# The short first load of an adaptive max-pool kernel, issued as two DMAs of 64 partitions from SyncE and ScalarE

## The chip, the cores and the metric

The kernel runs on one core of a Trainium2 chip. The metric is the device time of one execution in microseconds (us); lower is better. The profile shows the same execution from its first to its last instruction (the "span", some 1.8 us shorter). When the text speaks of "packet records", it means the list of single DMA packets in the trace, with start, duration, size and queue; the DMA engine is not recorded, so I give counts and means over all 16.

## The reference

The input has shape 32 x 256 x 4096, fp32 (134.22 MB). Each output is the maximum of 16 neighbouring values.

```python
for i in range(output_size):                 # 256
    start = int(i * length / output_size)    # 4096 / 256 = 16 values each
    end = int((i + 1) * length / output_size)
    result[:, :, i] = np.max(x[:, :, start:end], axis=-1)
```

There is one comparison for each value loaded, so the question is how fast 134 MB come in.

## The kernel before

The rows are spread over 128 partitions. A window is the 16 values of one output. SyncE loads chunks of 1024 windows per partition (8 MiB, 64 KiB to a partition) by turns into two places of one buffer, `ring`; each place is shifted by 152 windows for every second load into it. VectorE reduces each chunk in two parts, so that the place comes free early. The very first load is short: 128 windows, 1 MiB, 8 KiB to a partition. It lies in the gap between the two places.

```python
CHUNK, GAP, FIRST = 1024, 152, 128
...
ring = pool.tile([P, 2 * (CHUNK + GAP) * W], fp32, ...)     # W = 16
...
for n in loads:                    # 128, 1024, 1024, ... , the last 900
    xn = xg[:, a * W : (a + n) * W]
    if n == FIRST:
        nc.sync.dma_start(
            out=ring[:, CHUNK * W : (CHUNK + n) * W], in_=xn
        )
        pooled(dst, CHUNK, n)
    else:
        low = n_loads % 2 * (CHUNK + GAP)
        moved = n_loads // 2 % 2
        at = low + moved * GAP
        nc.sync.dma_start(out=ring[:, at * W : (at + n) * W], in_=xn)
        ...                        # two reductions, of 872 and 152 windows
...
nc.scalar.dma_start(out=og[:, full : full + last], in_=last_kept)
...                                # two larger stores, from SyncE
```

## Time and profile before

| what | value | where it is read |
|---|---|---|
| time | 334.97 us (334.9 to 335.02, 3 runs) | timed runs |
| DMA engines, SyncE's queue | 98.8% of the span | DMA queues |
| VectorE | 83% of the span | busy time |
| first DMA packet | 1.744 us | packet records |
| last DMA packet ends | 331.836 us | packet records |
| first reduction | 5.40 us, then 17.07 us of waiting | timeline |

The lines behind the table, and what they say of the bound, are in the prediction.

### The profile page before, as it was taken

How to read it: one execution, taken by the hardware profiler on the slowest of the kernel's cores; microseconds unless marked ns; L12 is line 12 of the kernel's file. 1: busy time of each engine (PE TensorE's matmuls, PEld its weight loads, DVE VectorE, ACT ScalarE, POOL GpSimd, SP SyncE). 2: the span in 40 equal slices, each digit the busy share in tenths (PEclk: the TensorE clock that was granted, in tenths of full speed). 3: DMA queues.
4: the chain of work that ended last, by engine and by line, in shares of the span. 5: the costliest groups of instructions: out<-in, count | busy, mean ns of one | idle time of the engine just before them, and what ended most of it. 6: DMA issues, size and time to landing. Idle time of an engine off the chain costs nothing.

```text
span 333.2 us, 113 instructions
## 1 busy us (share of the span) xinstructions
DVE 276.5 (83%) x32; POOL 0.2 (0%) x4
## 2 busy tenths in 40 slices
DVE  2009979797997979799797979979797998979993
POOL 0000000000000000000000000000000000000000
DMA  9898989899898989899898989899898989899987
GB/s 378 378 504 378 504 378 504 378 409 472 378 504 378 504 378 504 378 417 464 376 502 377 504 378 496 386 425 456 378 504 378 504 378 504 378 458 443 393 386 339
DMA packets 2880, 142.61 MB, mean 428 GB/s; under 512 B 320, under 2 KB 320, under 8 KB 448
## 3 DMA queue, kind: packets, MB, share of 16 engines
q1 hardware_dynamic: 2736, 142.15, 98.8%
q10 hardware_dynamic: 144, 0.46, 0.3%
HBM read 134.22 MB, written 8.39 MB: 428 GB/s over the span
## 4 chain that ended last, share of the span: by engine, by line
DMA 57%; DVE 36%; DVEq 5%; issue 0%; SPq 0%
DMA ring<-in_x_dram 57%; DVE kept L56 36%; DVEq L145 5%; SPq L85 0%
## 5 line engine op out<-in xcount | busy, mean ns | idle before, releaser
L56 DVE TENSOR_REDUCE kept<-ring 128x152 f32<-128x2432 f32 (+3 forms) x31 | 261.4, 8473 | 51.6 <-DMA ring<-in_x_dram 51.6
L56 DVE TENSOR_REDUCE ring<-ring 128x900 f32<-128x14400 f32 x1 | 15.1, 15141 | 0.0
L131 POOL MEMSET const-bfloat16-1.0<- 128x1 bf16 x1 | 0.1, 102 | 0.0
L131 POOL MEMSET const-uint8-127<- 128x1 uint8 x1 | 0.1, 101 | 0.0
L131 POOL MEMSET const-float32-0.0<- 128x1 f32 x1 | 0.1, 99 | 0.2 <-issue 0.2
L131 POOL MEMSET const-float32-1.0<- 128x1 f32 x1 | 0.1, 98 | 0.0
## 6 DMA issues: line engine op xcount, KB each, us to landing
ring<-in_x_dram SPq DMA_DIRECT2D x1, 8160.0 KB, 24.0
ring<-in_x_dram SPq DMA_DIRECT2D x1, 7200.0 KB, 21.6
out_dram<-kept SPq DMA_DIRECT2D x1, 4670.0 KB, 32.4
out_dram<-kept SPq DMA_DIRECT2D x1, 3072.0 KB, 18.1
ring<-in_x_dram SPq DMA_DIRECT2D x1, 1024.0 KB, 4.6
out_dram<-ring ACTq DMA_DIRECT2D x1, 450.0 KB, 4.2
ring<-in_x_dram SPq DMA_DIRECT2D x14, 24.0
```

The lines of the kernel that those rows point to most:

```text
L56: nc.vector.reduce_max(out=dst, in_=ring[:, at * W : (at + n) * W].rearrange("p (n w) -> p n w", w=W), axis=mybir.AxisListType.X,)
L131: nc = _bacc.Bacc("TRN2", target_bir_lowering=False, num_devices=1)
L145: with _tile.TileContext(nc) as tc:
```

## The change

The intent is to bring the short first load in sooner by issuing it from two engines at once, each for half of the partitions.

```diff
-                nc.sync.dma_start(
-                    out=ring[:, CHUNK * W : (CHUNK + n) * W], in_=xn
-                )
+                half = P // 2
+                for queue, h in ((nc.sync, slice(0, half)), (nc.scalar, slice(half, P))):
+                    queue.dma_start(
+                        out=ring[h, CHUNK * W : (CHUNK + n) * W], in_=xn[h]
+                    )
                 pooled(dst, CHUNK, n)
```

## The prediction

> **What bounds the kernel now.** I read the page first, then the table of busy time by stretches, then the chain of waits in order of time, then the timeline of the start and of one load in the middle. The page gives the shares:
>
> ```profile
> span 333.2 us, 113 instructions
> DVE 276.5 (83%) x32; POOL 0.2 (0%) x4
> DMA  9898989899898989899898989899898989899987
> q1 hardware_dynamic: 2736, 142.15, 98.8%
> HBM read 134.22 MB, written 8.39 MB: 428 GB/s over the span
> DMA ring<-in_x_dram 57%; DVE kept L56 36%; DVEq L145 5%; SPq L85 0%
> ```
>
> The transfers of the SyncE queue occupy the 16 DMA engines for 98.8% of the span, VectorE only 83%. The chain (last line) gives 57% to the loads and 36% to the reductions, which reads as if a faster reduction would help. The tail of the timeline says otherwise (start, length, what):
>
> ```profile
> 257.06 17.28 DVE L56 TENSOR_REDUCE kept<-ring 128x872 f32<-128x13952 f32 x2 [2.08 <-DMA ring<-in_x_dram]
> 271.77 19.68 SPq L94 DMA_DIRECT2D ring<-in_x_dram  x2
> 276.41 17.28 DVE L56 TENSOR_REDUCE kept<-ring 128x872 f32<-128x13952 f32 x2 [2.07 <-DMA ring<-in_x_dram]
> 295.75 17.28 DVE L56 TENSOR_REDUCE kept<-ring 128x872 f32<-128x13952 f32 x2 [2.07 <-DMA ring<-in_x_dram]
> ```
>
> A load lands every 19.35 us (276.41 - 257.06), VectorE works 17.28 of them and waits 2.07. The load issued at 271.77 lands at 295.73, 24 us later, though the rate is one per 19.35: for its first 4.6 us (to 276.41) it stands behind the load before it, whose landing starts the reduction at 276.41. So the DMA queue never runs dry, and the chain's reductions hide behind that backlog. The stretches (length, VectorE busy, POOL busy, clock, DMA share, GB/s) confirm it:
>
> ```profile
> 1.00:1.70 0.70, 0.00 (x0) 0.00 (x0) 1.00 0.00 0
> 1.70:5.00 3.30, 0.00 (x0) 0.00 (x0) 1.00 1.59 616
> 5.00:24.40 19.40, 2.29 (x1) 0.00 (x0) 1.00 1.01 436
> 63.00:295.70 232.70, 207.29 (x24) 0.00 (x0) 1.00 1.00 434
> 312.80:328.10 15.30, 15.29 (x2) 0.00 (x0) 1.00 0.99 428
> 331.90:333.20 1.30, 0.00 (x0) 0.00 (x0) 1.00 0.00 0
> ```
>
> (A packet counts in the stretch where it starts, hence 1.59 in the second row.) The engines are idle until 1.74 us, then saturated to 331.84 us, the end of the last packet. The time is therefore: start of the first packet (1.74), plus the DMA engines' work (330.1), plus the closing (1.3). A change counts only if it moves the first packet, or adds or removes DMA engine time.
>
> The first load, in the packet records of the trace: 128 packets of 8,192 B, eight per engine. The first packets start between 1.744 and 2.283 us and take 0.55 to 0.94 us, nearly all later ones 0.309 us (26.5 GB/s). The engines pass to the 64 KiB packets of the next load between 4.675 and 5.003 us; those take 2.418 us (27.1 GB/s). No gap lies between the two loads. Its consumer is far from critical:
>
> ```profile
> 0.73 0.38 SPq L85 DMA_DIRECT2D ring<-in_x_dram  x1
> 5.40 2.29 DVE L56 TENSOR_REDUCE kept<-ring 128x128 f32<-128x2048 f32 x1 [5.40 <-DMA ring<-in_x_dram]
> 24.75 17.28 DVE L56 TENSOR_REDUCE kept<-ring 128x872 f32<-128x13952 f32 x2 [17.07 <-DMA ring<-in_x_dram]
> ```
>
> VectorE starts on it at 5.40 and then waits 17.07 us for the next load.
>
> [...]one issue took 0.383 us on SyncE and 0.374 us on ScalarE, and the second SyncE issue already hides behind the first load. [...]The trace before has transfers of 128 partitions only, at 434 GB/s[...].
>
> **The change part by part.**
>
> Removed: half of the first SyncE transfer. The issues measured take 0.33 to 0.43 us whatever the size, so I save nothing there. SyncE's issue should still start at 0.73 and its next one near 1.16.
>
> Added: one issue on ScalarE, about 0.37 us. ScalarE is let go by the start barrier at 0.652, SyncE at 0.648, so the two go out together. Its later wait, for the final reduction, is untouched. Added too: 16 semaphore packets of 9 ns, one per engine: 0.01 us. The first reduction now waits for two semaphores, with 17 us of slack.
>
> Moved: the 1 MiB reaches each engine as two rings of four 8 KiB packets[...]. Bytes and data packets are unchanged. The first packet should still start at about 1.74, since it follows the SyncE issue. With no other effect the sum is 0.00 + 0.01 = no change: 335.0.
>
> [...]The engines' first packets are staggered by 0.31 us (15 of them, 1.744 to 2.055). Two engines half that list apart start some 0.16 us apart, which is half a packet. [...]As the engines never idle afterwards (the backlog above), such a delay goes to the end in full. Sum: 0.00 (issue) + 0.01 (semaphores)[...] = +0.9 us, so 334.97 + 0.9 = 335.9 us.[...]
>
> **The rivals.**
>
> Nothing moves. The queues alternate packet by packet[...].[...] The time is 334.9 to 335.1. I give it about 30%.
>
> Full serialization. The SyncE half goes first[...], the ScalarE half follows[...].[...] Against: from its fifth packet on, SyncE's ring already holds the 128-partition load[...]. The time is 336.8 to 337.4. About 20%.
>
> A faster start. The first packets cost 0.55 to 0.94 instead of 0.309 us. If the queues' start-ups overlap, or if ScalarE's is quicker, 0.1 to 0.4 us come off: 334.6 to 334.9. Against: the start-up is paid per engine, and all 16 are started by one issue already. About 12%.
>
> A late ScalarE half. If its small packets alternate with 64 KiB ones, each waits 2.4 us and the half lands after 10 to 14 us instead of 5.4. The first reduction starts late, but ends well before 24.7, and the third load, which overwrites this region, is issued only near 39.5. No change in the time by itself; it can go with any of the others.
>
> **Range and chances.** The lower end is a faster start of 0.3 us, the upper end full serialization: 334.6 to 337.3, centre 335.9. The runs before lie within 0.12 us, so noise is small. The 2% line is 6.7 us. The first load occupies the engines for 3.3 us in all, so even losing it whole or tripling it scarcely gets there. Chances: faster 0.005, same 0.99, slower 0.005.
>
> **What would show each step right or wrong.** The first packet stays within 0.1 us of 1.74 (issue saves nothing). The 8 KiB packets take clearly more than 0.309 us, 0.4 to 0.6[...]; if they stay at 0.309,[...] the time should be 335.0. The first 872-wide reduction, now at 24.75, starts 0.9 us later, and the same shift appears at 257.06, 276.41 and 295.75. VectorE still waits about 2.07 us ahead of each load. The queue of ScalarE carries about 1 MB instead of 0.46 MB, still under 1% share. The prediction is wrong if the shift at the start differs from the shift at the end, or if a later load loses its backlog.

The sum came to +0.9 us, 335.9 us in all. Its terms were 0.00 for the issue, 0.01 for the semaphores and 0.9 for slower 8 KiB packets. That third term was an estimate of mine, which started from eight packets at twice 0.309 us (+2.47 us, as a ceiling), took off the stagger of 0.16 us at each packet (+1.2 us left), and from that a quarter for the start-up (0.9). The doubling was not shown before the change; most of the changed kernel's packets later took 0.50 to 0.65 us. The 0.4 to 0.6 us named at the end of the prediction has the same ground.

## The result, and the profile after

The changed kernel took 337.47 us (median of 6 runs, 337.38 to 337.54) against 334.97 us: 2.50 us more. The ratio is 1.0074 (95% interval 1.0061 to 1.0087). Ratios here are the mean time of one kernel's runs over that of the other's in the same rounds, so they are not quite the ratio of the medians quoted. The loss is clear of the noise, below 2%, and 0.17 us above the upper end of the predicted range.

The page of the changed kernel, the lines that answer to the first fence of the prediction:

```profile
span 335.7 us, 116 instructions
DVE 276.5 (82%) x32; POOL 0.2 (0%) x4
DMA  8898989898989899998989898989898999999997
q1 hardware_dynamic: 2672, 141.62, 98.0%
q10 hardware_dynamic: 224, 0.99, 1.1%
HBM read 134.22 MB, written 8.39 MB: 425 GB/s over the span
DMA ring<-in_x_dram 58%; DVE kept L56 36%; DVEq L147 5%; SPq L87 0%
```

Same bytes, same VectorE time, still 99.1% of the engines' span (98.0 + 1.1; before, 98.8 + 0.3): yet the span is 2.5 us longer. So the DMA engines were busy for longer with the same bytes. Only a small part of the loss, 0.31 us, is a later start (below).

The timeline of the start (start, length, engine and line, what):

```profile
0.73 0.55 SPq L87 DMA_DIRECT2D ring<-in_x_dram  x1
0.73 0.55 ACTq L87 DMA_DIRECT2D ring<-in_x_dram  x1
1.33 60.39 SPq L96 DMA_DIRECT2D ring<-in_x_dram  x4
8.02 2.29 DVE L56 TENSOR_REDUCE kept<-ring 128x128 f32<-128x2048 f32 x1 [8.02 <-DMA ring<-in_x_dram]
27.32 17.28 DVE L56 TENSOR_REDUCE kept<-ring 128x872 f32<-128x13952 f32 x2 [17.02 <-DMA ring<-in_x_dram]
```

Both engines do issue at 0.73 us. But each issue takes 0.55 us instead of 0.38, the first reduction moves from 5.40 to 8.02 us, and the reduction after it from 24.75 to 27.32 us: 2.57 us late.

The timeline of the tail:

```profile
259.48 17.28 DVE L56 TENSOR_REDUCE kept<-ring 128x872 f32<-128x13952 f32 x2 [2.07 <-DMA ring<-in_x_dram]
278.83 17.28 DVE L56 TENSOR_REDUCE kept<-ring 128x872 f32<-128x13952 f32 x2 [2.08 <-DMA ring<-in_x_dram]
298.20 17.28 DVE L56 TENSOR_REDUCE kept<-ring 128x872 f32<-128x13952 f32 x2 [2.08 <-DMA ring<-in_x_dram]
```

They stood at 257.06, 276.41 and 295.75 us: 2.42 to 2.45 us late, with the waits unchanged. So nearly all of the loss arises before 27 us and is only carried along from there. The stretches (length, VectorE busy, POOL busy, clock, DMA share, GB/s), two of those that the prediction shows:

```profile
1.70:5.00 3.30, 0.00 (x0) 0.00 (x0) 1.00 0.93 218
63.00:295.70 232.70, 207.83 (x25) 0.00 (x0) 1.00 1.00 433
```

Up to 5 us it is 218 GB/s at a DMA share of 0.93; before, it was 616 at 1.59. Both old figures include the 64 KiB packets that had already started by 5 us, so they do not compare rate with rate; what they show is that the large load had not begun. Later on, the rate is as before (433 against 434).

The packet records give the rest:

| us from the span's start | before | after | difference |
|---|---|---|---|
| first packet of all | 1.744 | 2.057 | +0.31 |
| first 64 KiB packet, mean start of 16 | 4.865 | 6.803 | +1.94 |
| first 64 KiB packet, mean end of 16 | 7.283 | 9.667 | +2.38 |
| last packet of all, end | 331.836 | 334.248 | +2.41 |

The durations of all packets, summed and divided by 16 engines, rise from 330.36 to 332.41 us: +2.05. With the later first packet (+0.31) that makes 2.36 of the 2.41. The 8 KiB packets, 0.309 us each before, begin in the same way, but from about the fourth one on most take 0.50 to 0.65 us. An engine's order, put together from ends and next starts, is four packets of SyncE, four of ScalarE, and only then the first 64 KiB packet, which takes 2.63 to 3.00 us instead of 2.42.

### The profile page after: what moved, and what is told of

It is laid out like the page before. It is cut to its first block, busy times and chain, and to the rows that moved or that the text cites. A ratio compares the mean times of both kernels' runs of the same rounds, so it can differ in the third digit from the quotient of the medians.

```text
span 335.7 us, 116 instructions
## 1 busy us (share of the span) xinstructions
DVE 276.5 (82%) x32; POOL 0.2 (0%) x4
## 4 chain that ended last, share of the span: by engine, by line
DMA 58%; DVE 36%; DVEq 5%; SPq 0%; issue 0%
DMA ring<-in_x_dram 58%; DVE kept L56 36%; DVEq L147 5%; SPq L87 0%
```

## The experiments

The theory after the result, called P in what follows, is that of the prediction at its full size: while a transfer covers only partitions 0 to 63 or only 64 to 127, or a quarter within one of these halves, all 16 DMA engines run at half rate (the ceiling of 2.47 us for this 1 MiB); partitions 32 to 95 together it holds to be as fast as all 128. Why that should be so no run shows; the runs test what P says of the partitions. Its rivals: Q, two queues at work at once cost; S, each extra or smaller transfer costs; L, two engines that issue at once start late. Edits are shown against the changed kernel, unless said otherwise. Each run gave the correct result.

### both_on_sync: the same halves, one queue

```diff
-for queue, h in ((nc.sync, slice(0, half)), (nc.scalar, slice(half, P))):
+for queue, h in ((nc.sync, slice(0, half)), (nc.sync, slice(half, P))):
```

> The two 64-partition halves stay, but SyncE issues both, one behind the other. Theory P ([...]its 8 KiB packets take about 0.62 us instead of 0.309): the packets stay at about 0.6 us and the time at 336.9 to 337.5. Theory Q (the loss comes from two queues sharing the DMA engines): packets back to 0.31, time 335.0 to 335.3. Theory L (what matters is that two engines issue at once, which made the first packet 0.31 us late): the issue is back at about 0.38 us and the first packet at 1.74 us, which takes 0.3 us off, whatever P does.

Measured: 337.41 us (337.31 to 337.47, 4 runs), ratio 1.0072 (1.0057 to 1.0087). The packets are as slow as in the changed kernel (median 0.61 us). Without ScalarE the loss is the same, so Q falls. So does L: SyncE alone takes 0.542 us for the first issue and the first packet still comes at 2.041 us. The later start belongs to this form of transfer and not to two engines issuing at once. My expectation of an issue of 0.38 us was wrong.

### split_by_columns: two queues, all partitions in each

```diff
-half = P // 2
-for queue, h in ((nc.sync, slice(0, half)), (nc.scalar, slice(half, P))):
-    queue.dma_start(out=ring[h, CHUNK * W : (CHUNK + n) * W], in_=xn[h])
+half = n * W // 2
+lo = CHUNK * W
+for queue, c in ((nc.sync, 0), (nc.scalar, half)):
+    queue.dma_start(out=ring[:, lo + c : lo + c + half], in_=xn[:, c : c + half])
```

> SyncE and ScalarE each issue one transfer at the same time, as in the change, but each covers all 128 partitions and half of the columns: 4 KiB packets, eight to an engine and transfer. P: [...]a 4 KiB packet takes 0.15 to 0.17 us, and only the late start of 0.3 us remains: 335.0 to 335.5. Q, or theory S (two transfers instead of one, or smaller ones, are what costs): 336.5 or more.

Measured: 335.09 us (335.0 to 335.23, 4 runs), ratio 1.0003 (0.9987 to 1.002): the same as before. A 4 KiB packet took 0.159 us. The timeline of the start:

```profile
0.73 0.40 ACTq L88 DMA_DIRECT2D ring<-in_x_dram  x1
0.73 0.38 SPq L88 DMA_DIRECT2D ring<-in_x_dram  x1
5.67 2.29 DVE L56 TENSOR_REDUCE kept<-ring 128x128 f32<-128x2048 f32 x1 [5.67 <-DMA ring<-in_x_dram]
24.98 17.28 DVE L56 TENSOR_REDUCE kept<-ring 128x872 f32<-128x13952 f32 x2 [17.03 <-DMA ring<-in_x_dram]
```

Two engines issue at once, and each issue takes 0.38 to 0.40 us; the first packet comes at 1.740 us. Two queues and smaller packets cost nothing that can be told from noise. S falls in its general form, and L a second time. But there is no gain either: the reduction starts at 5.67 us, no earlier than the 5.40 us of before.

### middle_half: 64 partitions from both halves

```diff
-for queue, h in ((nc.sync, slice(0, half)), (nc.scalar, slice(half, P))):
+for queue, h in (
+    (nc.sync, slice(32, 96)),
+    (nc.scalar, slice(0, 32)),
+    (nc.scalar, slice(96, P)),
+):
```

> SyncE loads partitions 32 to 95, again 64 of them, and ScalarE the two outer quarters (0 to 31 and 96 to 127), one after the other. [...]P: the 64 packets of SyncE take about 0.31 us after the first ones, the 64 of ScalarE about 0.62;[...] time 336.0 to 336.6. S or a rule that 64 partitions are slow as such: the SyncE packets take about 0.6 us too and the time is 337.4 or more.

Measured: 336.19 us (336.11 to 336.41, 4 runs), ratio 1.0037 (1.0022 to 1.0052): half the loss, as P says. The packet durations did not sort themselves as neatly as I expected. ScalarE's first quarter went ahead (first packet at 1.716 us), and its packets were still short; in the middle part the first two of each engine were slow (0.57 and 0.49 us in the mean), the third took 0.33, and the fourth, which mostly came behind a packet of ScalarE's last quarter, 0.53. It looks as if a slow part shows in the records one or two packets later. That is a reading, not a proof, so the test was repeated below with packets eight times as large.

### whole_on_scalar: the whole first load from ScalarE

Against the kernel before:

```diff
-nc.sync.dma_start(out=ring[:, CHUNK * W : (CHUNK + n) * W], in_=xn)
+nc.scalar.dma_start(out=ring[:, CHUNK * W : (CHUNK + n) * W], in_=xn)
```

> The whole first load, 128 partitions, from ScalarE alone, while SyncE starts with the first large load at the same time. P: packets at 0.309 us, time 334.9 to 335.4. Q: over 336. L: both issues take about 0.55 us and the first packet comes at about 2.05 instead of 1.74 us, so 335.2 to 335.4; without L the issues stay at about 0.38 us and the time at 335.0. If the large load gets ahead, the first reduction starts only near 24 us, which the third load's backlog of some 3 us should absorb.

Measured: 337.52 us (336.91 to 338.28, 4 runs), ratio 1.0077 (1.0061 to 1.0092). None of the theories is about what happened here. P and L had the time wrong. Q named over 336 us, and that figure came out, but not for its reason: both_on_sync had cost as much with one queue, and in this run, with both queues at work, the small packets kept their 0.309 us and the 64 KiB packets from the second round to the tenth their 2.418. The issues took 0.39 and 0.38 us and the first packet came at 1.736 us (L falls a third time). But the large load got ahead, and the small packets were let in one after each 64 KiB packet, until about 25 us (the rounds of 64 KiB packets lie 2.72 to 2.73 us apart, which is 2.418 + 0.309):

```profile
25.58 36.66 DVE L56 TENSOR_REDUCE kept<-ring 128x128 f32<-128x2048 f32 x5 [25.58 <-DMA ring<-in_x_dram]
65.44 17.28 DVE L56 TENSOR_REDUCE kept<-ring 128x872 f32<-128x13952 f32 x2 [3.20 <-DMA ring<-in_x_dram]
```

The reduction of the first large load began at 27.79 instead of 24.75 us, behind the small one. The third load was issued about 3 us later for it, and its reduction waited 3.20 us instead of 2.07. The packet records show the DMA engines partly idle near 44 us (by the number of packets in flight, 0.59 us in the mean of 16 engines from 3 to 330 us, against 0.01 before), and the first sixteen 64 KiB packets took 3.09 us in the mean. So the backlog of "some 3 us", which I had counted on, was used up. The profiled execution is the fastest of the four (336.91 us); what made the others up to 1.4 us slower is not recorded. This run does not test P's slow packets, as every transfer in it has 128 partitions. It does show that a late first load is not free here; the changed kernel escaped it, since its halves landed before the large load.

### quarters_on_sync: four transfers of 32 partitions

```diff
-half = P // 2
-for queue, h in ((nc.sync, slice(0, half)), (nc.scalar, slice(half, P))):
-    queue.dma_start(out=ring[h, CHUNK * W : (CHUNK + n) * W], in_=xn[h])
+for q in range(0, P, 32):
+    h = slice(q, q + 32)
+    nc.sync.dma_start(out=ring[h, CHUNK * W : (CHUNK + n) * W], in_=xn[h])
```

> SyncE issues the first load as four quarters of 32 partitions in order[...]. Theory P[...]: packets slow to about 0.6 us once the start is over. The quarters' issues should take 0.36 us instead of 0.55 and the first packet should come at 1.72 instead of 2.05 us, as with the 32-partition issues of the run before. If the late first packet is a part of the loss of its own, the time is 337.1, 0.3 below the two halves[...]. Theory S (a cost for each extra transfer): 338.5 or more, as there are now three extra ones.

Measured: 337.05 us (337.02 to 337.13, 4 runs), ratio 1.0062 (1.0047 to 1.0077). Four transfers cost less than two, so it is not the count (S). The first issue took 0.382 us and the first packet came at 1.740 us. What is left, 337.05 - 334.97 = 2.08 us, is about the loss by slow packets alone (three more issues and their semaphore packets are in it too). The 0.36 us up to both_on_sync fits the 0.30 us by which the halves start later (2.041 against 1.740).

### large_two_queues and large_one_queue: eight times the size

The first load is whole again, and the 8 MiB load after it is split instead. In the second run `nc.scalar` is `nc.sync`. Against the kernel before:

```diff
-nc.sync.dma_start(out=ring[:, at * W : (at + n) * W], in_=xn)
+if n_loads == 0:
+    half = P // 2
+    for queue, h in ((nc.sync, slice(0, half)), (nc.scalar, slice(half, P))):
+        queue.dma_start(out=ring[h, at * W : (at + n) * W], in_=xn[h])
+else:
+    nc.sync.dma_start(out=ring[:, at * W : (at + n) * W], in_=xn)
```

> The first load is whole again; the load after it, 8 MiB, is split by partition halves, one from SyncE and one from ScalarE, as in the change but eight times as large. Full serialization[...] costs 8 x 8 x 0.302 = 19.3 us: 354.3. A fixed cost for each split (late start, extra issue) would leave it at 335 to 338. [...]the loss lies between: with engines wholly out of step 335 to 337.

> As the run with two queues, but both 4 MiB halves of the large load come from SyncE, one behind the other. No taking of turns is possible, so theory P with full serialization has 354.3, whatever the two-queue run does. A fixed cost for each split: 335 to 338. If this is far above the two-queue run, taking turns helps; if both are the same, engines stay in step or the queues serve the halves one after the other.

Measured: 355.6 us (355.42 to 355.72, 4 runs), ratio 1.0615 (1.0599 to 1.063), with two queues; 356.46 us (356.32 to 356.58, 4 runs), ratio 1.0642 (1.0624 to 1.066), with one. The losses are 20.6 and 21.5 us. The loss grows with the bytes, so it is no fixed cost of a split. It is even somewhat above the 19.3 us of exactly half the rate (eight packets per engine, 2.418 us more for each).

In the run with two queues the queues did take turns, as the case in between of my expectation supposed, and it hardly helped. The packet records show the sixteen packets of each round all from the same queue: ScalarE twice at the start, then SyncE and ScalarE by turns, and SyncE twice at the end. The sixteen starts of a round lie within 0.63 us, so no engine got a whole packet ahead of another: all were on the same half. After the first round, a packet took 4.93 to 4.96 us where the half had just changed, and 5.11 to 5.12 where it had not; before, it took 2.418. Worked out for sixteen packets of 64 KiB, that is 205 GB/s at 5.12 us and 212 at 4.94, against 434 at 2.418. The run with one queue has 5.12 us and, at its one change of half, 4.92. So a change of half took some 0.17 to 0.20 us off a packet, and the four more changes with two queues make up the difference between the two profiled runs (0.67 us of packet time per engine, 355.6 against 356.32 us).

### large_middle: the middle part at the large size

Against the kernel before, SyncE only:

```diff
-nc.sync.dma_start(out=ring[:, at * W : (at + n) * W], in_=xn)
+if n_loads == 0:
+    for h in (slice(32, 96), slice(0, 32), slice(96, P)):
+        nc.sync.dma_start(out=ring[h, at * W : (at + n) * W], in_=xn[h])
+else:
+    nc.sync.dma_start(out=ring[:, at * W : (at + n) * W], in_=xn)
```

> The large load is again issued by SyncE alone and in parts of at most 64 partitions, but the first part is partitions 32 to 95, then come 0 to 31 and 96 to 127. The split in one queue at partition 64 cost 21.5 us. Theory P[...]: the four packets per engine of the middle part take about 2.42 us, the four of the two quarters about 4.9 to 5.1; half of the loss, 345.4 to 346.0. If transfers of fewer than 128 partitions are slow whatever the partitions: about 356, all packets near 5 us.

Measured: 345.68 us (345.56 to 345.75, 4 runs), ratio 1.0316 (1.0301 to 1.0332), beside 335.07 us for the kernel before in these rounds. That is 10.6 us, half of the 21.5. The stretches of this run:

```profile
8.00:14.00 6.00, 0.00 (x0) 0.00 (x0) 1.00 0.81 350
20.00:26.00 6.00, 0.00 (x0) 0.00 (x0) 1.00 0.83 175
26.00:32.00 6.00, 0.00 (x0) 0.00 (x0) 1.00 0.85 175
32.00:38.00 6.00, 2.16 (x1) 0.00 (x0) 1.00 0.88 350
```

and the same stretches of large_one_queue:

```profile
8.00:14.00 6.00, 0.01 (x1) 0.00 (x0) 1.00 0.85 175
20.00:26.00 6.00, 0.00 (x0) 0.00 (x0) 1.00 0.88 186
32.00:38.00 6.00, 0.00 (x0) 0.00 (x0) 1.00 0.85 175
```

The figures jump in steps, as each counts whole rounds of 64 KiB packets that start in it (350 is two rounds in 6 us, 175 one). But in the first stretch, with the DMA share alike, the middle part moves twice as much. By the packet records, the first four packets of each engine took 2.418 us in the mean and the next four 4.62, 5.12, 4.94 and 5.12. The first packet of the next load still took 2.84 us: the tail of the slow phase seems to be booked there, as in the changed kernel. Bytes, packet size, queue and engine count are alike in the two runs; they differ in which partitions are written together (and in one transfer more). Of the theories tested, P alone fits. What is shown is that the choice of partitions decides: 2.418 us a packet for 32 to 95, and 4.62 to 5.12 for the two outer quarters. Why it decides, the trace does not record. One rival stays untested: each partition has its own row of the input, so the rows read together change with the partitions. It would have to say why 64 neighbouring rows are slow from row 0 and fast from row 32.

### large_columns: the two queues at the large size

Against the kernel before:

```diff
-nc.sync.dma_start(out=ring[:, at * W : (at + n) * W], in_=xn)
+if n_loads == 0:
+    half = n * W // 2
+    for queue, c in ((nc.sync, 0), (nc.scalar, half)):
+        queue.dma_start(
+            out=ring[:, at * W + c : at * W + c + half],
+            in_=xn[:, c : c + half],
+        )
+else:
+    nc.sync.dma_start(out=ring[:, at * W : (at + n) * W], in_=xn)
```

> The large load split in two halves by columns, from SyncE and ScalarE, each over all 128 partitions: 32 KiB packets, the same bytes per transfer and the same two queues as the run that cost 20.6 us. P: packets of 1.21 us,[...] 334.9 to 335.3; the first load may land some us late, as its queue takes turns, at no cost. If two queues at work at once cost something at this size, it shows here: above 337.

Measured: 335.24 us (335.15 to 335.31, 4 runs), ratio 1.0005 (0.9989 to 1.0022), so the same as before. One stretch of this run, to be laid beside those above:

```profile
8.00:14.00 6.00, 0.00 (x0) 0.00 (x0) 1.00 1.01 437
```

A 32 KiB packet took 1.213 us. The first load did land late (its reduction started at 15.35 us) as the queues took turns; that cost nothing, being done before the large load had landed. At 8 MiB, then, splitting by columns over two queues cost nothing that these runs can tell from noise, and splitting by partition halves over the same two queues cost 20.6 us.

No variant beat the kernel before. That agrees with its profile: the DMA engines are full from 1.744 us to the end, and no split takes bytes away.

## Why the prediction was wrong

- **What bounds the kernel: right.** A delay at the start came through to the end almost unchanged (2.57 us at the second reduction, 2.42 to 2.45 in the tail, 2.50 in the time), and VectorE's waits in the tail stayed at 2.07 to 2.08 us. Why the shift shrinks from 2.57 to some 2.43 us was not looked into.
- **Where the cost lies: right.** Which partitions are written together costs the time: large_middle (10.6 us lost, against 21.5 with the cut at partition 64) and large_columns (335.24 us, no loss) show it, and quarters_on_sync (2.08 us lost) shows it free of the later start. The reason that the prediction gave for it was not shown.
- **The size of the packet term: wrong, and this is the step that failed.** The prediction put the ceiling at 2.47 us and went on that the two queues are not in step. From a stagger of 0.16 us it took the eight packets down to 1.2 us of loss, and with the start-up to 0.9. The runs show 2.05 us of additional packet time in its place, or 2.08 in the time of quarters_on_sync. What failed is the premise that each engine would mix the two halves, so that the stagger would help with every packet. Each engine did SyncE's four packets first and then ScalarE's four: the half changed once. At that change two packets took 0.586 and 0.536 us in place of 0.612 (means of 16), together 0.10 us less, where the prediction took 0.16 off each of eight. Of the 0.42 us between the ceiling of 2.47 and the 2.05 measured, that leaves about 0.3 for the start-up, which is what I had allowed (an estimate from these sums). In large_two_queues, where the halves did alternate, a change took 0.17 us off a 64 KiB packet, so the 0.16 itself is near what was seen; whether 8 KiB packets that alternate would have kept the loss near 1 us, no run tested.
- **The start: wrong.** "The first packet should still start at about 1.74." It started at 2.057: a 64-partition issue took 0.55 us in place of 0.38, and the first packet came 0.31 us later. I had taken issue times to be independent of the shape, because the profile before has 128-partition transfers only. This term of 0.00 measured 0.31.
- **The sum.** 0.31 + 2.05 is 2.36, and the end of the last packet moved by 2.41. In the span it is 2.5. The small rest (about 0.1) was not tested.
- **Slips in its readings.** One of the sixteen first packets, the one at 2.283 us, took 0.43 us, so the range is 0.43 to 0.94 and not 0.55 to 0.94. The closing is 333.20 - 331.84 = 1.36 us, not 1.3, and the three terms give the span of 333.2 us, not the time, which is 1.8 us longer. ScalarE's queue held 1.1%, not under 1%. None of these moves the sum.
- **The rivals.** Full serialization came nearest (336.8 to 337.4), and its order, SyncE's half first and ScalarE's after it, is the one that the packet records show. What I held against it, that SyncE's fifth packet would already belong to the large load, did not happen: no 64 KiB packet started on an engine before its ScalarE packets were through. Nothing moved only in the column splits; a faster start, of 0.1 us or more, was seen in no run.

What stays open: why packets of one half took 5.12 us and not twice 2.418 = 4.84; why an issue for 64 partitions took longer (0.53 to 0.58 us) than one for 128 (0.38 to 0.40) or for 32 (0.36 to 0.38; first issue of an engine each), and why a 128-partition issue that followed one of 64 on SyncE was slow too (0.56 to 0.61 us, against 0.425 for the second issue before); and why ScalarE's half came after all of SyncE's in the changed kernel, when in the column split it began within 0.76 us.

## What to carry to other kernels

In this kernel, whose DMA engines are full from the first packet to the last, a second issuing engine brought nothing, and what counted was which partitions a transfer covers. Splitting by columns was free (335.09 and 335.24 us); splitting at partition 64 about halved the rate of the split bytes (4.92 to 5.12 us per 64 KiB packet against 2.418), whether from one queue or two, and that came out in the time: 2.5 us for 1 MiB (0.3 of them a later start), over 20 us for 8 MiB. If partitions must be split, measure which parts are slow (32 to 95 ran at full rate, 2.418 us a packet; 0 to 31 with 96 to 127, one after the other, did not, at 4.62 to 5.12), and don't count on two queues filling in for each other (20.6 us lost with two, 21.5 with one).
